# Sums of weight blocks for the MLP's down projection, made by DMAs in device memory

## The chip, the cores and the metric

The kernel runs on one core of one Trainium2 chip. The core has a matrix engine (TensorE, "PE" in the profile; its weight loads are "PEld"), a vector engine (VectorE, DVE), an activation engine (ScalarE, ACT), a general engine (GpSimd, POOL) and a sync engine (SyncE, SP), and 16 DMA engines that all of them share. The metric is the time of one execution on the device, in microseconds (us), lower is better. The change is compared by the median of several runs on the same chip.

## The reference

Two layers, each with attention and an MLP, on 256 tokens of width 1024, in float32. The attention (sparse heads and forgetting heads beside each other) is unchanged here. What the change is about is the MLP:

```
h = _rms_norm(x, g_pre_mlp[l])
y = jnp.square(jax.nn.relu(h @ w_up[l])) @ w_down[l]
x = x + _rms_norm(y, g_post_mlp[l])
```

`w_up` is 1024 x 4096 and `w_down` 4096 x 1024 for each layer.

## The kernel before

**Precision.** Every large product is made of three: a weight is split into a rounded part (`whi`) and the rest (`wlo`), the activations too, and high x high, high x low and low x high are added in PSUM (`mm3`, line 819; each is one matmul of 512 columns in the down projection). The splitting of a weight costs a ScalarE copy (`whi`) and a VectorE subtraction (`wlo`). Some weights, of kind "cast", are split by two DMAs of GpSimd's queue instead, with a ScalarE negation between them (`Weights.cast`, line 589; tile `whic`).

**The units.** All weights stand in one list of units in the order of use (lines 690 to 744): for a layer the six chunks of `w_in` (`("in", c, q)`), eight of `w_out` (`("out", k)`), four of the first up columns, and then, for the MLP, up blocks and rows of `w_down` in turn. Each unit is 512 KB as a rule. SyncE loads them into nine buffers with the tag "raw" (`Weights.load`, line 580), up to 12 units ahead. `Weights.get` (line 604) returns a unit's two parts.

**The MLP.** `up_block` (line 1607) makes 128 hidden columns for all 256 tokens with 8 matmuls of 512 columns and 8 of 256. ScalarE copies half of the PSUM result to `h`, VectorE adds the other half, and `squared` (line 1620) applies a relu and a square on ScalarE. The down projection goes through the hidden columns in pairs of 128-row blocks (loop at line 1735). A pair's four weight blocks and four activation blocks form a 2 x 2 by 2 x 2 block product. The letter N in `PAIRS` (line 100) marks a pair with eight block products, S one with seven, made from sums and differences of the blocks (a Strassen-like scheme). Each layer has 14 such pairs, the first of them N, the others S; the last two pairs of blocks go to `down` directly (line 1776). For an S pair, `operands` (line 1631) makes the activation sums, and `Weights.pair` (line 631) the weight sums: `s` = upper row's two blocks + block b12 of the lower row (one VectorE add of 128 x 1024, line 657), and from it two more (lines 659 and 660). The seven products add up in seven PSUM banks over all pairs; in the last pair `bank_sums` (line 1714) combines the banks as their products end.

**The order.** Nothing is issued in program order. `Recorder` (line 237) records all operations of the program, `schedule` (line 378) simulates the engines with a cost table, and each engine's order is what that simulation gives; an operation's rank is a due time, to which `SHIFTS` (line 38) adds random amounts from listed seeds for listed ranges of operations (`shift`, line 373). On each engine, and on each queue, what is issued later waits behind what is issued earlier. GpSimd's own work is small: its DMAs for cast weights in the MLP and, in attention, the masks of the forget bias (`forget_bias`, line 1203).

Of the kernel before, what the change touches and what calls it, by code (L numbers as in the profile page):

```python
# [17 lines left out]

F32 = mybir.dt.float32
# [17 lines left out]
CAST_HEAD, CAST_TAIL = 1900, 3000.0  # L37
SHIFTS = ((628313922, 3237, 3426, 150),
          (701981142, 3624, 4129, 150),
          (295680985, 724, 994, 400),  # L40
          (1009766576, 3675, 3950, 2500),
          (651636505, 4766, 4926, 1000),
          (434429208, 2775, 3180, 150),
          (330988171, 2766, 2894, 400),
          (958370765, 1025, 1090, 1000),
          (602402177, 3152, 3215, 1000),
          (332536528, 4058, 4926, 400),
          (79554178, 1086, 1213, 2500),
          (824043290, 940, 1079, 1000),
          (929176947, 3864, 4015, 400),  # L50
          (947144828, 4255, 4300, 2500),
          (756884776, 3456, 3727, 2500),
          (352764400, 4430, 4926, 150),
          (731199972, 4142, 4926, 150),
          (788198929, 2312, 2374, 150),
          (633381528, 3971, 4127, 400),
          (189321402, 212, 298, 1000),
          (1057377739, 3585, 3670, 1000),
          (849038195, 2001, 2686, 150),
          (171135740, 3547, 3803, 1000),  # L60
          (797947262, 3731, 4006, 150),
          (383419172, 3908, 4049, 150),
          (230125934, 3754, 4926, 400),
          (705380179, 934, 1003, 1000),
          (185781734, 312, 351, 400),
          (109646568, 3638, 4033, 1000),
          (284246459, 1248, 1293, 2500),
          (664160879, 3832, 3909, 1000),
          (490562272, 1162, 1214, 2500),
          (375550898, 420, 479, 1000),  # L70
          (587899166, 421, 510, 400),
          (501883715, 407, 453, 1000),
          (769019964, 3494, 3544, 2500),
          (369012694, 3554, 3595, 1000),
          (68297707, 3532, 3570, 2500),
          (889231503, 306, 456, 150),
          (1002206527, 1055, 1198, 1000),
          (976623511, 478, 553, 400),
          (608331619, 372, 417, 1000),
          (308090406, 341, 392, 1000))  # L80
LANDING = 2500.0
# [17 lines left out]
            "share", "x0", "x1", "fV", "hs", "cs", "pcT", "vbig", "vS", "vW", "kstk", "kstv", "rT")  # L99
PAIRS = ("NSSSSSSSSSSSSS",) * 2  # L100
DCAST = 1
EPS = 1e-6

CHUNKS = [(512, 1024), (1024, 1312), (0, 512), (1312, 1824), (1824, 2336), (2336, 2848)]
# [132 lines left out]
class Recorder:  # L237
# [135 lines left out]
    def shift(self, seed, a, b, size):  # L373

        for op, x in zip(self.ops[a:b], np.random.default_rng(seed).standard_normal(b - a)):
            op.rank += size * x * (0.01 if op.engine == "tensor" else 1.0)
# [196 lines left out]
class Weights:  # L573


    def __init__(self, nc, tile, units):
        self.nc, self.tile, self.units = nc, tile, units
        self.raw, self.marks, self.ring, self.w1 = {}, [], None, 1

    def load(self, i):  # L580
        kind, shape, src = self.units[i]
        if kind == "raw":
            self.w1 = 1 - self.w1
            self.raw[i] = self.tile([P] + shape, F32, name="w1", tag=f"act{self.w1}", bufs=2)
        else:
            self.raw[i] = self.tile([P] + shape, F32, name="wraw", tag="raw", bufs=RBUFS)
        self.nc.sync.dma_start(self.raw[i], src)

    def cast(self, i):

        nc, marks = self.nc, self.marks
        kind, shape, src = self.units[i]
# [5 lines left out]
        nc.gpsimd.dma_start(hi, src)  # L598
        nc.scalar.activation(lo, hi.bitcast(F32), AF.Copy, scale=-1.0)
        nc.gpsimd.dma_start(lo, src.bitcast(F32R), accum_op=OP.add)  # L600
        nc.key = None
        return hi, lo

    def get(self, i):
# [16 lines left out]
        for j in range(shape[0]) if i < len(FIRSTS) else [slice(None)]:  # L621
            if i > 1:
                nc.scalar.activation(hi[:, j], raw[:, j], AF.Copy)
            else:

                nc.vector.tensor_copy(hi[:, j], raw[:, j])
            nc.vector.tensor_sub(lo[:, j], raw[:, j], hi[:, j].bitcast(F32))
        nc.key = None
        return hi, lo

    def pair(self, i, seven):

        nc, marks = self.nc, self.marks
        for x in (i, i + 1):
            assert len(marks) == x
            marks.append(len(nc.ops))
            if x not in self.raw:
                nc.key = marks[max(x - LOAD_LEAD, 0)]
                self.load(x)
        above, below = (self.raw.pop(x)[:, 0] for x in (i, i + 1))  # L640
        nc.key = marks[max(i - SPLIT_LEAD, 0)]

# [36 lines left out]
def trunk(nc, A, consts_in, out, sbp, pp, dram):  # L679
# [6 lines left out]
    def small(shape, name, bufs=2):  # L686
        return tile(shape, F32, name=name, tag=name, bufs=bufs)
# [17 lines left out]
    for l in range(DEPTH):  # L705
# [22 lines left out]
        def add_up(fc, q):  # L728
            add_unit((l, "up", fc, q), [8, P], A["w_up"][l, 4 * (fc - 1) + q], "cast" if q % 2 else "split")

        def add_down(fc, q, kind):
            add_unit((l, "dn", fc, q), [1, D], wd[:, 4 * fc + q:4 * fc + q + 1, :], kind)

        for u in range(16):
            b, shared = u % 2 * 2, u < len(PAIRS[l])
            if u + 2 < 16 and shared:
                add_up((u + 2) // 2, b)
            if u == len(PAIRS[l]):
                for v in range(4 + 2 * u, 32):
                    add_up(v // 4, v % 4)  # L740
            for i in range(2):
                add_down(u // 2, b + i, "cast" if not shared and (u < 14 or i == DCAST) else "split")
            if u + 2 < 16 and shared:
                add_up((u + 2) // 2, b + 1)

    W = Weights(nc, tile, units)

# [193 lines left out]
    for l in range(DEPTH):  # L941
# [665 lines left out]
        def up_block(fc, b, h):  # L1607
# [106 lines left out]
        def bank_sums(p):  # L1714
# [17 lines left out]
            elif p == 3:  # L1732
                nc.vector.tensor_add(banks[3], banks[3], sums[5])

        for u in range(len(PAIRS[l])):
            fc, b = (u + 2) // 2, u % 2 * 2
            if fc < 8:
                h = tokt("h")
                up_block(fc, b, h)
            if u == 0:  # L1740
                acts.update(enumerate(then()))
            if u == 1:
# [3 lines left out]
            if PAIRS[l][u] == "S":  # L1746
                b11, b22, b21, t1, t2, t3, t4 = w
                work = [(1, 1, b11), (2, 3, b21), (3, 6, b22), (5, 5, t1), (7, 4, t2), (6, 0, t3), (4, 2, t4)]
                if u == len(PAIRS[l]) - 1:
                    work = [work[i] for i in (0, 5, 3, 4, 6, 1, 2)]  # L1750
            else:
                b11, b22, b21, b12 = w
                work = [(2, 1, b11), (4, 0, b11), (5, 0, b12), (3, 4, b12), (2, 3, b21), (4, 2, b21), (5, 2, b22), (3, 5, b22)]
            for n, (p, x, v) in enumerate(work):
                if n == 4 and fc < 8:
                    up_block(fc, b + 1, h)
                    if u + 2 < len(PAIRS[l]):
                        q = blocks(u + 2)
                        squared(q[0][:, 0:4].rearrange("p a n -> p (a n)"), h)
                        acts[u + 2] = operands(u + 2, q)  # L1760
                    else:
                        direct_operands(u + 2, h)
                new = p not in banks
# [5 lines left out]
        ys = {(1, 0): banks[2], (1, 1): banks[3], (0, 0): banks[4], (0, 1): banks[5]}  # L1769
        for v in range(2 + len(PAIRS[l]), 16):  # L1770
            h = tokt("h")
            for i in range(2):
                up_block(v // 2, v % 2 * 2 + i, h)
            direct_operands(v, h)

# [82 lines left out]
```

## Time and profile before

| | |
|---|---|
| median of 3 runs | 598.09 us (598.0 to 598.14) |
| span of the profiled execution | 596.4 us |
| its clock of TensorE, mean | 0.999 |
| device memory read | 132.37 MB |
| device memory written | 1.07 MB |
| mean DMA rate over the span | 225 GB/s |

The profiled execution's own time outside the span isn't listed; the median lies 1.7 us over the span. In rows of the profile, "a<-b" means that the operation writes tile a from tile b; every operation stands at line 498, where the recorded program is emitted, so groups are told apart by their tiles. A row of stretches (such as "579.00:590.00") has the length, the busy time and number of instructions of PE, PEld, DVE, ACT and POOL, the granted clock of TensorE, the DMA engines' mean busy share, and GB/s. The stretches of the layers, by TensorE's products: attention of layer 0 to about 125 us, its MLP to about 297 us, attention of layer 1 to about 420 us, its MLP to 590 us.

### The profile page before, as it was taken

How to read it: one execution, taken by the hardware profiler on the slowest of the kernel's cores; microseconds unless marked ns; L12 is line 12 of the kernel's file. 1: busy time of each engine (PE TensorE's matmuls, PEld its weight loads, DVE VectorE, ACT ScalarE, POOL GpSimd, SP SyncE). 2: the span in 40 equal slices, each digit the busy share in tenths (PEclk: the TensorE clock that was granted, in tenths of full speed). 3: DMA queues.
4: the chain of work that ended last, by engine and by line, in shares of the span. 5: the costliest groups of instructions: out<-in, count | busy, mean ns of one | idle time of the engine just before them, and what ended most of it. 6: DMA issues, size and time to landing. Idle time of an engine off the chain costs nothing.

```text
span 596.4 us, 9853 instructions
## 1 busy us (share of the span) xinstructions
PE 589.1 (99%) x3308; PEld 492.1 (83%) x3308; DVE 542.1 (91%) x1206; ACT 461.4 (77%) x902; POOL 54.0 (9%) x84
## 2 busy tenths in 40 slices
PE   9999999999999999999999999999999999999995
PEld 7978887788888888888888888777888888888884
DVE  6899999879999999998899999986999999999974
ACT  6797878678897787888698658985878878878762
POOL 0001100110011010111000020001100101011110
PEclk9999999999999999999999999999999999999999
DMA  8998128778888989897856481557868899898352
GB/s 315 401 407 290 63 75 293 258 221 222 262 240 270 257 229 281 259 248 211 265 190 234 143 296 59 174 180 248 183 240 240 251 259 232 261 270 220 70 107 70
DMA packets 39858, 134.08 MB, mean 225 GB/s; under 512 B 4704, under 2 KB 5888, under 8 KB 39808
## 3 DMA queue, kind: packets, MB, share of 16 engines
q1 hardware_dynamic: 30592, 99.90, 48.3%
q0 software_dynamic: 9216, 33.56, 25.2%
q8 instruction: 26, 0.43, 0.3%
q14 instruction: 24, 0.20, 0.1%
HBM read 132.37 MB, written 1.07 MB: 224 GB/s over the span
## 4 chain that ended last, share of the span: by engine, by line
PE 98%; DMA 1%; DVE 0%; DVEq 0%; ACT 0%; issue 0%
PE s L498 42%; PE acc L498 26%; PE x L498 20%; PE o L498 10%; DMA first<-in_first_dram 1%; DVE x L498 0%; DVE m L498 0%; DVEq L1854 0%; ACT rl L498 0%; DVE whi L498 0%; DVE rsqrt L498 0%; DVE gcol L498 0%
## 5 line engine op out<-in xcount | busy, mean ns | idle before, releaser
L498 DVE TENSOR_TENSOR wlo<-wraw,whi 128x1024 fp32r<-128x1024 f32 (+2 forms) x156 | 171.1, 1104 | 9.9 <-ACT whi L498 8.4
L498 ACT ACTIVATE whi<-wraw 128x1024 fp32r<-128x1024 f32 (+2 forms) x156 | 149.4, 966 | 29.1 <-PE s L498 13.1
L498 PE MATMUL s<-xT,whic 128*128 128x512 f32 (+1 forms) x448 | 84.0, 336 | 0.0
L498 PEld LDWEIGHTS s<-xT,whic 128*128 128x128 f32 x448 | 72.8, 189 | 10.9
L498 POOL DMA_DIRECT2D whic<-in_w_up_dram x56 | 40.2, 720 | 348.3 <-PE s L498 132.9
L498 DVE TENSOR_TENSOR wlo<-wsum,whi 128x1024 fp32r<-128x1024 f32 x52 | 62.6, 1218 | 1.7 <-ACT whi L498 1.5
L498 ACT ACTIVATE whi<-wsum 128x1024 fp32r<-128x1024 f32 x52 | 53.8, 1054 | 8.2 <-PE acc L498 7.7
L498 PE MATMUL s<-xT,whi 128*128 128x512 f32 x224 | 56.9, 390 | 0.0
L498 PEld LDWEIGHTS s<-xT,whi 128*128 128x128 f32 x224 | 41.8, 188 | 8.5
L498 ACT ACTIVATE attn<-attn,st 128x256 f32<-128x256 f32 (+1 forms) x96 | 42.8, 448 | 5.1 <-DVE st L498 4.7
L498 PE MATMUL x<-whi,aS 128*128 128x512 f32 x120 | 46.4, 390 | 0.0
L498 PE MATMUL acc<-whi,aS 128*128 128x512 f32 x120 | 43.0, 391 | 0.0
L498 ACT ACTIVATE h<-s 128x256 f32<-128x256 f32 x56 | 21.4, 382 | 23.4 <-PE s L498 23.1
L498 PE MATMUL s<-whi,aS 128*128 128x512 f32 x104 | 37.9, 392 | 0.0
L498 PE MATMUL acc<-whi,xT 128*128 128x512 f32 (+1 forms) x128 | 36.2, 349 | 0.0
L498 DVE TENSOR_TENSOR wsum<-wraw,wsum 128x512 f32<-128x512 f32 x52 | 35.5, 683 | 0.1
L498 PE MATMUL x<-whi,xT 128*128 128x512 f32 x112 | 34.7, 391 | 0.3 <-DVE gcol L498 0.3
L498 ACT ACTIVATE whic<-whic 128x1024 fp32r<-128x1024 f32 x32 | 33.5, 1049 | 1.0 <-DMA whic<-in_w_up_dram 1.0
L498 PE MATMUL acc<-xT,whi 128*128 128x512 f32 x128 | 34.1, 398 | 0.0
L498 PEld LDWEIGHTS s<-xT,wlo 128*128 128x128 f32 x224 | 31.2, 190 | 2.5
L498 PE MATMUL s<-xT,wlo 128*128 128x256 f32 x224 | 32.3, 283 | 0.0
L498 DVE TENSOR_TENSOR wsum<-wraw 128x1024 f32<-128x1024 f32 x26 | 31.6, 1216 | 0.0
(236 smaller groups left out, 1321.1 us busy)
## 6 DMA issues: line engine op xcount, KB each, us to landing
wraw<-in_w_down_dram SPq DMA_DIRECT2D x60, 512.0 KB, 5.1
whic<-in_w_up_dram POOLq DMA_DIRECT2D x56, 512.0 KB, 7.1
wraw<-in_w_in_dram SPq DMA_DIRECT2D x36, 512.0 KB, 6.5
wraw<-in_w_up_dram SPq DMA_DIRECT2D x36, 512.0 KB, 4.5
wraw<-in_w_out_dram SPq DMA_DIRECT2D x16, 512.0 KB, 5.2
w<-in_cmp_w_k_dram SPq DMA_DIRECT2D x8, 512.0 KB, 8.2
w<-in_cmp_w_v_dram SPq DMA_DIRECT2D x8, 512.0 KB, 8.9
whic<-in_w_down_dram POOLq DMA_DIRECT2D x8, 512.0 KB, 6.6
```

The lines of the kernel that those rows point to most:

```text
L498: getattr(getattr(self.nc, op.engine), name)(*[real(v) for v in args], **{k: real(v) for k, v in kw.items()})
```

## The change

For some S pairs the sum `s` is made in device memory. `PRE` lists pairs with the weight unit at whose splitting the sum is begun: in layer 0 pairs 0 to 5 from `("in", 5, 1)` to `("out", 2)`, in layer 1 pairs 0 to 11 from `("in", 4, 0)` to `("out", 3)`. Only pairs with the letter S are taken (pair 0 is N), so 5 and 11 sums. At a listed unit GpSimd copies one element of that unit's `wlo` (so its queue waits until the split is done), then issues the accumulation of the sum begun before (b12, read twice, added to both halves), then the copy of this pair's upper row to device memory. In the MLP SyncE loads the sum into a "raw" buffer, and of the lower row only the first half; the VectorE add at line 657 is left out for these pairs. For the other S pairs it stays.

Besides: `up_block`'s add becomes a custom VectorE operation that adds and clamps to the range from 0 to the largest float, so `squared` needs no relu (28 ScalarE operations fewer); the last pair's products come in another order; `SHIFTS` is another list, 11 entries where there were 43. `CASTS`, `HWCAST` and `AHEAD` have values that keep the former behaviour, and the rewritten loops over the up blocks make the same units and products in the same recorded order.

```diff
-SHIFTS = ((628313922, 3237, 3426, 150),
...
+SHIFTS = ((1003350174, 1078, 1222, 2500),
...
+PRE = ([(0, ('in', 5, 1)), (1, ('in', 5, 2)), (2, ('in', 5, 3)), (3, ('out', 0)), (4, ('out', 1)), (5, ('out', 2))], [(0, ('in', 4, 0)), (1, ('in', 4, 1)), (2, ('in', 4, 2)), (3, ('in', 4, 3)), (4, ('in', 5, 0)), (5, ('in', 5, 1)), (6, ('in', 5, 2)), (7, ('in', 5, 3)), (8, ('out', 0)), (9, ('out', 1)), (10, ('out', 2)), (11, ('out', 3))])
...
+    def presum(self, i, seen):
+
+        nc = self.nc
+        nc.gpsimd.tensor_copy(self.tick, seen)
+        nc.after = nc.ops[-1]
+        if self.begun:
+            j, s = self.begun.pop()
+            b12 = self.units[j + 1][2][:, 0, 512:]
+            nc.gpsimd.dma_start(s, bass.AP(b12.tensor, b12.offset, [b12.ap[0], [0, 2], b12.ap[1]]), accum_op=OP.add)
+        if i is not None:
+            s = self.sums[i] = nc.tile(self.dram, [P, 2, 512], F32, name=f"sum{i}")
+            nc.gpsimd.dma_start(s, self.units[i][2][:, 0].rearrange("p (a n) -> p a n", a=2))
+            self.begun.append((i, s))
+        nc.after = None
...
-        self.nc.sync.dma_start(self.raw[i], src)
+        self.nc.sync.dma_start(*[x[:, :, :512] if half else x for x in (self.raw[i], src)])
...
+        if i in self.pre or self.begun:
+            self.presum(self.pre.get(i), lo[0:1, 0, 0:1].bitcast(F32))
...
+        made = seven and i in self.sums
+        if made:
+            nc.key = marks[max(i + 1 - LOAD_LEAD, 0)]
+            s = self.tile([P, 2, 512], F32, name="wsum", tag="raw", bufs=RBUFS)
+            nc.sync.dma_start(s, self.sums.pop(i))
...
-        s, z = (self.tile([P, 2, 512], F32, name="wsum", tag="kx%d" % j) for j in range(2))
-        nc.vector.tensor_add(s, above.rearrange("p (a n) -> p a n", a=2), b12[:, None, :].to_broadcast([P, 2, 512]))
+        z = self.tile([P, 2, 512], F32, name="wsum", tag="kx1")
+        if not made:
+            s = self.tile([P, 2, 512], F32, name="wsum", tag="kx0")
+            nc.vector.tensor_add(s, above.rearrange("p (a n) -> p a n", a=2), b12[:, None, :].to_broadcast([P, 2, 512]))
...
+    pre = {}
+    for l in range(DEPTH):
+        for u, at in PRE[l]:
+            if PAIRS[l][u] == "S":
+                pre[index[(l,) + at]] = index[l, "dn", u // 2, u % 2 * 2]
...
-            nc.vector.tensor_add(d, ps[:, :S], d)
+            nc.vector._custom_dve(op=TENSOR_ADD_SAT, out=d, in0=ps[:, :S], in1=d, s0=FMAX, s1=0.0)
...
-            rl = small([P, 512], "rl")
-            nc.scalar.activation(rl, h, AF.Relu)
-            nc.scalar.activation(d, rl, AF.Square)
+            nc.scalar.activation(d, h, AF.Square)
...
-                    work = [work[i] for i in (0, 5, 3, 4, 6, 1, 2)]
+                    work = [work[i] for i in (0, 5, 1, 3, 4, 6, 2)]
```

More of the change, by code (lines that the diff above doesn't have):

```diff
@@ L17 @@
 from concourse import mybir
+from concourse.dve_ops import TENSOR_ADD_SAT
 F32 = mybir.dt.float32
@@ L37 @@
 CAST_HEAD, CAST_TAIL = 1900, 3000.0
-SHIFTS = ((628313922, 3237, 3426, 150),
[L39 to L80, printed above, removed]
+SHIFTS = ((1003350174, 1078, 1222, 2500),
+          (534435998, 190, 301, 1000),
+          (1036816610, 3033, 3605, 1000),
+          (52205258, 1084, 1186, 1000),
+          (344636226, 190, 635, 400),
+          (407487018, 190, 243, 400),
+          (68684986, 3533, 3578, 2500),
+          (-1, 3555, 3556, -3362),
+          (363124729, 2994, 3063, 400),
+          (811001117, 3517, 3622, 1000),
+          (68206210, 3819, 3828, 2500))
 LANDING = 2500.0
@@ L99 @@
             "share", "x0", "x1", "fV", "hs", "cs", "pcT", "vbig", "vS", "vW", "kstk", "kstv", "rT")
-PAIRS = ("NSSSSSSSSSSSSS",) * 2
+PAIRS = ('NSSSSSSSSSSSSS', 'NSSSSSSSSSSSSS')
+CASTS = ((1, 3), (1, 3))
+HWCAST = 0
+PRE = ([(0, ('in', 5, 1)), (1, ('in', 5, 2)), (2, ('in', 5, 3)), (3, ('out', 0)), (4, ('out', 1)), (5, ('out', 2))], [(0, ('in', 4, 0)), (1, ('in', 4, 1)), (2, ('in', 4, 2)), (3, ('in', 4, 3)), (4, ('in', 5, 0)), (5, ('in', 5, 1)), (6, ('in', 5, 2)), (7, ('in', 5, 3)), (8, ('out', 0)), (9, ('out', 1)), (10, ('out', 2)), (11, ('out', 3))])
 DCAST = 1
 EPS = 1e-6
+AHEAD = 0
+FMAX = 3.4028234663852886e38
 CHUNKS = [(512, 1024), (1024, 1312), (0, 512), (1312, 1824), (1824, 2336), (2336, 2848)]
@@ L373, in shift @@
     def shift(self, seed, a, b, size):
+        if seed < 0:
+            for op in self.ops[a:b]:
+                op.rank += size
+            return
         for op, x in zip(self.ops[a:b], np.random.default_rng(seed).standard_normal(b - a)):
@@ L573, with __init__, load @@
 class Weights:
-    def __init__(self, nc, tile, units):
-        self.nc, self.tile, self.units = nc, tile, units
+    def __init__(self, nc, tile, units, dram, pre):
+        self.nc, self.tile, self.units, self.dram, self.pre, self.sums, self.begun = nc, tile, units, dram, pre, {}, []
+        self.tick = tile([1, 1], F32, name="tick")
         self.raw, self.marks, self.ring, self.w1 = {}, [], None, 1
-    def load(self, i):
+    def presum(self, i, seen):
[11 more added lines that the diff above has]
+        nc.after = None
+    def load(self, i, half=False):
         kind, shape, src = self.units[i]
@@ L597, in cast @@
         nc.key = marks[max(i - CAST_LEAD, 0)]
-        nc.gpsimd.dma_start(hi, src)
-        nc.scalar.activation(lo, hi.bitcast(F32), AF.Copy, scale=-1.0)
+        if HWCAST:
+            self.load(i)
+            raw = self.raw.pop(i)
+            nc.scalar.activation(lo, raw, AF.Copy, scale=-1.0)
+            nc.scalar.activation(hi, raw, AF.Copy)
+        else:
+            nc.gpsimd.dma_start(hi, src)
+            nc.scalar.activation(lo, hi.bitcast(F32), AF.Copy, scale=-1.0)
         nc.gpsimd.dma_start(lo, src.bitcast(F32R), accum_op=OP.add)
@@ L638, in pair @@
                 nc.key = marks[max(x - LOAD_LEAD, 0)]
-                self.load(x)
+                self.load(x, half=seven and i in self.sums and x == i + 1)
         above, below = (self.raw.pop(x)[:, 0] for x in (i, i + 1))
+        made = seven and i in self.sums
[3 more added lines that the diff above has]
+            nc.sync.dma_start(s, self.sums.pop(i))
         nc.key = marks[max(i - SPLIT_LEAD, 0)]
@@ L728, in add_up @@
         def add_up(fc, q):
-            add_unit((l, "up", fc, q), [8, P], A["w_up"][l, 4 * (fc - 1) + q], "cast" if q % 2 else "split")
+            add_unit((l, "up", fc, q), [8, P], A["w_up"][l, 4 * (fc - 1) + q], "cast" if q in CASTS[l] else "split")
         def add_down(fc, q, kind):
             add_unit((l, "dn", fc, q), [1, D], wd[:, 4 * fc + q:4 * fc + q + 1, :], kind)
+        ups = [(1 + j // 4, j % 4) for j in range(28)]
+        for x in ups[:AHEAD]:
+            add_up(*x)
         for u in range(16):
             b, shared = u % 2 * 2, u < len(PAIRS[l])
[L736 to L740, printed above, removed]
+            for x in ups[AHEAD + 2 * u:AHEAD + 2 * u + 1]:
+                add_up(*x)
             for i in range(2):
                 add_down(u // 2, b + i, "cast" if not shared and (u < 14 or i == DCAST) else "split")
-            if u + 2 < 16 and shared:
-                add_up((u + 2) // 2, b + 1)
-    W = Weights(nc, tile, units)
+            for x in ups[AHEAD + 2 * u + 1:AHEAD + 2 * u + 2]:
+                add_up(*x)
+    pre = {}
[3 more added lines that the diff above has]
+                pre[index[(l,) + at]] = index[l, "dn", u // 2, u % 2 * 2]
+    W = Weights(nc, tile, units, dram, pre)
     def weight(*key):
@@ L1733, in bank_sums, with up @@
                 nc.vector.tensor_add(banks[3], banks[3], sums[5])
-        for u in range(len(PAIRS[l])):
[L1736 to L1741, printed above, removed]
+        hs = {}
+        def up(j):
+            if j >= 28:
+                return
+            if j % 2 == 0:
+                hs[j // 2] = tokt("h")
+            up_block(1 + j // 4, j % 4, hs[j // 2])
+            if j == AHEAD:
+                acts.update(enumerate(then()))
+            if j % 2:
+                u = j // 2 + 2
+                if u < len(PAIRS[l]):
+                    q = blocks(u)
+                    squared(q[0][:, 0:4].rearrange("p a n -> p (a n)"), hs[j // 2])
+                    acts[u] = operands(u, q)
+                else:
+                    direct_operands(u, hs[j // 2])
+        for j in range(AHEAD):
+            up(j)
+        for u in range(len(PAIRS[l])):
+            b = u % 2 * 2
+            up(AHEAD + 2 * u)
             if u == 1:
@@ L1754, in trunk @@
             for n, (p, x, v) in enumerate(work):
[L1755 to L1762, printed above, removed]
+                if n == 4:
+                    up(AHEAD + 2 * u + 1)
                 new = p not in banks
@@ L1769, in trunk @@
         ys = {(1, 0): banks[2], (1, 1): banks[3], (0, 0): banks[4], (0, 1): banks[5]}
[L1770 to L1774, printed above, removed]
         def down(t, n, k, w):
```

## The prediction

> **What bounds the kernel now.** I read the page first: the span, the busy times, the chain that ended last.
>
> ```profile
> span 596.4 us, 9853 instructions
> PE 589.1 (99%) x3308; PEld 492.1 (83%) x3308; DVE 542.1 (91%) x1206; ACT 461.4 (77%) x902; POOL 54.0 (9%) x84
> PE 98%; DMA 1%; DVE 0%; DVEq 0%; ACT 0%; issue 0%
> ```
>
> TensorE is busy 99% of the span and the chain is TensorE for 98% of it. But a matmul's end is modelled, so busy does not yet mean that it runs at its rate. The waits of TensorE and the first and last long pieces of the chain come next (start, length, engine and tile, matmuls).
>
> ```profile
> PE o L498 <- PEq L1848: 0.8, 1, 0.8
> PE x L498 <- DVE gcol L498: 0.3, 1, 0.3
> ...
> 4.94 11.56 PE x L498 x48
> ...
> 584.75 5.45 PE acc L498 x24
> ```
>
> It waits 1.1 us in all. The products run from 4.94 us to 590.20 us, 585.3 us; 4.9 us lie ahead (the first load) and 6.2 us behind (norm and store). The change touches neither end. What is left is the rate in between. Here are the same up block in layer 0's MLP, six pairs apart, the product behind it, and the last stretch by engine.
>
> ```profile
> 208.70 2.93 PE L498 MATMUL s<-xT,whic 128*128 128x512 f32 x16
> 211.47 0.40 PE L498 MATMUL s<-whi,aS 128*128 128x512 f32 x1
> ...
> 270.78 2.93 PE L498 MATMUL s<-xT,whic 128*128 128x512 f32 x16
> ...
> 579.00:590.00 11.00, 11.00 (x50) 8.93 (x48) 5.93 (x13) 3.92 (x12) 0.00 (x0) 1.00 0.08 24
> ```
>
> In the last 11 us VectorE works 5.93 us, ScalarE 3.92 us, the DMA engines 8%, and the granted clock is 1.00: nothing there can hold TensorE up. There 24 products of 512 columns take 5.45 us, 227 ns each: I take this as the rate. An up block takes 211.47 - 208.70 = 2.77 us. A pair of seven products with its two up blocks is then 7 x 3 x 0.227 + 2 x 2.77 = 10.31 us. The measured period is (270.78 - 208.70) / 6 = 10.347 us. So **0.04 us per pair, 1 us over the 26 seven-product pairs of both layers, is all that a faster VectorE or ScalarE can give back in the MLP.**
>
> By the Trainium skill (TensorE: Matmul & The Clock Gate, "Wait — 56ns, not 53.3ns?") a warm matmul of 512 columns starts 215.7 ns after the one before. This trace disagrees: 227 ns at full clock, even beside idle engines. Were the 11 ns contention that lighter engines remove in the changed pairs, an estimate by the page would be 16 x 37 x 11 ns = 6.5 us less; by the row, where VectorE and ScalarE do about half of what they do in the MLP and the products stay at 227 ns, it is 0, and I go by the row.
>
> **The change part by part.** The listed pairs are six in layer 0 and twelve in layer 1; each list's first is pair 0, whose letter is N and which the code skips. So 5 + 11 = 16 sums are made, not the 17 of the heading. The products stay seven (eight for pair 0) per pair: TensorE's work is unchanged.
>
> ```profile
> L498 DVE TENSOR_TENSOR wsum<-wraw 128x1024 f32<-128x1024 f32 x26 | 31.6, 1216 | 0.0
> L498 ACT ACTIVATE rl<-h 128x512 f32<-128x512 f32 x28 | 17.3, 617 | 4.0 <-DVE h L498 3.9
> L498 DVE TENSOR_TENSOR h<-s,h 128x256 f32<-128x256 f32 x56 | 23.5, 419 | 3.3 <-ACT h L498 2.7
> L498 DVE CUSTOM_DVE_ANT_0 attn<-x,cst 128x256 f32<-128x256 f32 x32 | 13.3, 417 | 0.4 <-PE s L498 0.4
> ```
>
> Removed: 16 adds of 1216 ns, 19.5 us of VectorE, all in the MLP, and 28 relus of 617 ns, 17.3 us of ScalarE, also there. Both lie beside TensorE, which does not wait for them: at most the 1 us above comes out. I take 0.3 us, a third, since not each lag of a few ns is theirs.
>
> Changed: 56 plain adds become clamping adds, a custom operation that this trace does not have. Another custom operation on the same 128x256 takes 417 ns against 419. Lower end 0; upper end two passes, 56 x 0.42 = 24 us of VectorE. I take 0, by the row of the same size.
>
> Added on the DMA side: per sum a copy of 512 KB from device memory to device memory and an accumulating DMA of 512 KB into it. Later one 512 KB load of the sum, and 256 KB less of the lower row.
>
> ```profile
> q1 hardware_dynamic: 30592, 99.90, 48.3%
> q0 software_dynamic: 9216, 33.56, 25.2%
> ...
> 66.00:100.00 34.00, 34.00 (x215) 27.50 (x216) 32.20 (x119) 28.54 (x87) 0.77 (x2) 1.00 0.41 136
> 100.00:140.00 40.00, 40.00 (x244) 31.68 (x241) 33.68 (x98) 29.50 (x75) 3.55 (x5) 1.00 0.79 234
> ...
> 327.00:376.00 49.00, 49.00 (x359) 40.54 (x357) 47.35 (x155) 34.68 (x89) 3.66 (x8) 1.00 0.48 167
> 376.00:409.00 33.00, 33.00 (x229) 25.11 (x224) 25.82 (x103) 26.88 (x80) 0.26 (x1) 1.00 0.59 191
> 440.00:480.00 40.00, 40.00 (x203) 34.08 (x202) 37.77 (x55) 32.06 (x50) 4.30 (x6) 1.00 0.76 220
> 480.00:520.00 40.00, 40.00 (x207) 34.23 (x206) 39.31 (x58) 32.19 (x43) 5.77 (x8) 1.00 0.90 257
> 520.00:560.00 40.00, 40.00 (x204) 34.16 (x204) 39.17 (x55) 31.62 (x42) 5.74 (x8) 1.00 0.81 208
> ```
>
> GpSimd's queue (q0) moved 64 transfers of 512 KB in 25.2% of 596.4 us: 2.35 us of all 16 engines each. SyncE's (q1) takes 48.3% x 596.4 / 99.90 = 2.88 us per MB, 1.51 us for 512 KB. The trace has no transfer that reads and writes device memory in bulk. Lower end for one: 1.51 us; upper end: 2 x 2.35 us, if both sides count. I take 2.35 us, the queue's own row, so 4.7 us per sum (3.0 to 9.4): 23.5 us in layer 0, **52 us in layer 1** (33 to 103).
>
> Each sum starts when VectorE has split the weight that the list names. Counted back from the first 512-column split (pair 1's, which follows them in the units' order), the first and last of these splits are, for layer 0 and layer 1:
>
> ```profile
> 66.27 1.22 DVE L498 TENSOR_TENSOR wlo<-wraw,whi 128x1024 fp32r<-128x1024 f32 x1
> ...
> 92.72 1.21 DVE L498 TENSOR_TENSOR wlo<-wraw,whi 128x1024 fp32r<-128x1024 f32 x1
> ...
> 327.19 1.23 DVE L498 TENSOR_TENSOR wlo<-wraw,whi 128x1024 fp32r<-128x1024 f32 x1
> ...
> 375.72 1.21 DVE L498 TENSOR_TENSOR wlo<-wraw,whi 128x1024 fp32r<-128x1024 f32 x1
> ```
>
> Free DMA time is one minus the last column but one, times the length. In layer 0 it is 20.1 + 8.4 = 28.5 us from 66 to 140 us: 23.5 us fit. In layer 1 it is 25.5 + 13.5 = **39 us** from 327 to 409, for 52: 13 us of transfers are still to do when the MLP's cast weights begin. The MLP has 9.6 + 4.0 + 7.6 = 21 us free from 440 to 560, of which its larger loads take 11 x 0.75 = 8 us (256 KB each): 13 us are left, so it comes out even at the end. Who waits behind the sums?
>
> ```profile
> 416.85 1.82 POOL L498 DMA_DIRECT2D whic<-in_w_up_dram x2 [6.45 <-ACT whic L498]
> ...
> 436.28 1.77 PE L498 MATMUL s<-xT,whic 128*128 128x512 f32 x7
> ...
> 411.85 0.33 SPq L498 DMA_DIRECT2D wraw<-in_w_down_dram  x1
> 422.16 0.33 SPq L498 DMA_DIRECT2D gains<-in_g_post_mlp_dram  x1
> ...
> whic<-in_w_up_dram POOLq DMA_DIRECT2D x56, 512.0 KB, 7.1
> ...
>   DMA wraw<-in_w_out_dram: 0.6, 1
>   DMA wraw<-in_w_in_dram: 0.5, 2
> ```
>
> On GpSimd's queue it is the first cast weights of layer 1. Their second half is issued at 416.85, lands 7.1 us later by the median, at 424, and is first used at 436.28: 12 us to spare, against 13 us of arrears. On SyncE's queue nothing is issued from 411.85 to 422.16, as no buffer comes free, and in the whole run work on loaded weights waited 1.1 us for a load: these loads are early, by some 10 us, and can give way to the casts. Against the change speaks the Trainium skill (DMA: Bandwidth & Descriptors, "Issuing engines are not separate DMA queues"): transfers of all engines run on the same 16. The shares above agree, near 0.9 in the MLP where both queues work. By that rule the sums take their time from weight loads, and only spare time pays for them.
>
> So the sums cost 0 while 12 + 10 us of cover stand against 13; beyond that, the cost is what is late.
>
> The GpSimd side: each sum adds a one-element copy that waits for VectorE's split of a weight, and behind it stand its two DMAs and, in attention, the 16 masks of the forget bias, which the fox scores need.
>
> ```profile
> POOL bias L498 <- ACT attn L498: 65.9, 1, 65.9
> ...
> 106.56 0.48 PE L498 MATMUL x<-whi,oT 128*128 128x512 f32 x1
> 106.97 0.93 PE L498 MATMUL s<-fkT,fqT 64*128 64x128 f32 x8
> ...
> 576.66 0.70 DVE L498 TENSOR_TENSOR x<-x,s 128x512 f32<-128x512 f32 x1
> ...
> 579.15 0.39 PE L498 MATMUL x<-whi,aT 128*128 128x512 f32 x1
> ```
>
> GpSimd is busy 9% and stands idle 65.9 us before a mask; a copy ahead of it costs nothing unless its weight is later than the mask's turn. Lower end 0, upper end one weight's spacing, 5 us; I take 0.
>
> The sums' load on SyncE waits for the accumulation, and all later loads stand behind it. The planner places the load by when its data is due; I take 0, and if a sum is late, the cost is its lateness.
>
> Last pair: bank 2's products move ahead, so bank 4's sum (0.70 us) ends later before the product that reads it (576.66 + 0.70 against 579.15, 1.8 us spare). Three products, 0.68 us, move away: still covered. 0, at worst 0.7 us twice.
>
> The order: the list of shifts that the planner adds to its ranks is another, so all engines' orders change. The change of tile between products is what an order can save or waste: 106.97 - 106.56 = 0.41 us against 0.227, 0.18 us. About 20 groups of small products enter and leave it, 40 changes, 4 to 7 us in the span. A reorder that merges or parts a fifth moves the time by about 1 us, either way. I take 0.
>
> Sum: 0 - 0.3 + 0 = 0.3 us less: a span of 596.1 us. The median of the runs shown, 598.09, lies 1.7 us over the span; that stays, so **597.8 us**.
>
> **The rivals.**
>
> *The order comes out better.* The 1 us of the MLP and 1 to 2 us of tile changes in attention: 2 us, 596 us. For it: such lags exist. Against: TensorE is at its rate nearly everywhere, so little is left.
>
> *The sums crowd the DMA engines (slower).* Place: layer 1, 409 to 450 us, the cast weights behind eleven sums. It decides from (39 + 22) / 11 = 5.5 us per sum, against my 4.7. At 5.9 us TensorE waits 0.4 x 11, about 4 us: 602 us. For it: most of the way between my bounds lies above. Against: 5.5 us is a sixth over the queue's own row, and a share of 0.5 counts packets that wait.
>
> *The order comes out worse.* More tile changes, a mask behind a waiting copy: 2 us, 600 us.
>
> *The clamping add takes two passes.* Layer 0 has 8 MLP pairs without relief; VectorE, at 39.3 of 40 us in such stretches, gets 0.84 us more per 10.35 and sets the pace: 0.7 us each, near 5 us in all: 603 us.
>
> *The sums are not made as described:* 16, not 17, which is 1.2 us of VectorE off the chain, no time.
>
> **How the numbers follow.** A measurement here tells 0.2%, 1.2 us, from no change: same is 596.9 to 599.3. No change worth telling 0.43; better order 0.30, so faster 0.30; crowded DMAs 0.15, worse order 0.10, slow clamp 0.02, slower 0.27. The range goes from 595.6 (the order's best case and a bit) to 602.5 (crowding as priced): about 0.08 lies below and 0.08 above.
>
> **What would show it.** Right: TensorE's rows at 227 ns and 10.3 us per pair, ten adds of wsum left, no rl beside h, VectorE some 20 us and ScalarE 17 us less busy, the DMA share near 1 from 327 to 440 us, the time unmoved. Wrong: waits of TensorE on cast weights or splits after 410 us; h at 0.8 us; products under 220 ns; an attention that is shorter or longer by over 1.5 us.

## The result: 602.76 us, and where 4.4 us come from

| | before | after |
|---|---|---|
| median of the runs | 598.05 us (598.0 to 598.14, 4 runs) | 602.76 us (601.95 to 602.93, 4 runs) |
| ratio to before | | 1.0073 [1.0061, 1.0085] |
| span of the profiled execution | 596.4 us | 600.8 us |
| its clock of TensorE, mean | 0.999 | 0.994 |

The changed kernel is slower by 0.7%. That is 0.26 us above the upper end of the predicted range and on the side that had a chance of 0.27. The medians differ by 4.7 us, the spans of the two profiled executions by 4.4; the account below is of the spans. All operations of the changed kernel stand at line 476.

The page of the kernel after first: span, busy times, the two DMA queues (packets, MB, share of 16 engines), the chain, and three rows of the DMA issues (KB each, median us to landing).

```profile
span 600.8 us, 9926 instructions
PE 591.2 (98%) x3308; PEld 494.7 (82%) x3308; DVE 526.6 (88%) x1190; ACT 447.2 (74%) x874; POOL 82.9 (14%) x134
...
q1 hardware_dynamic: 32896, 104.09, 48.2%
q0 software_dynamic: 14080, 50.34, 36.0%
...
PE 95%; DMA 4%; ACT 0%; DVE 0%; issue 0%; DVEq 0%
...
sum<-in_w_down_dram POOLq DMA_DIRECT2D x32, 512.0 KB, 12.2
wraw<-in_w_out_dram SPq DMA_DIRECT2D x16, 512.0 KB, 10.0
```

VectorE is 15.5 us less busy and ScalarE 14.2 us less, somewhat under the forecast 20 and 17. But DMA has gone from 1% to 4% of the chain: somewhere a load now sets the end. The 32 `sum` transfers are two for each of 16 sums. The groups of VectorE of the kernel after show the other two edits at the sizes that were expected, 10 adds left of 26 and a clamping add of 420 ns:

```profile
L476 DVE CUSTOM_DVE_ANT_0 h<-s,h 128x256 f32<-128x256 f32 x56 | 23.3, 420 | 4.3 <-ACT h L476 3.7
L476 DVE TENSOR_TENSOR wsum<-wraw 128x1024 f32<-128x1024 f32 x10 | 12.2, 1217 | 0.0
```

Next, in which stage the time is lost. In the chain (start, length, what) the same 16 products stand at the end of layer 0 and at the end of layer 1's attention. Before:

```profile
292.29 3.63 PE acc L498 x16
...
414.31 3.63 PE acc L498 x16
```

After, with the first and the last products:

```profile
5.27 11.75 PE x L476 x48
...
292.69 3.63 PE acc L476 x16
...
419.09 3.64 PE acc L476 x16
...
589.87 4.77 PE acc L476 x21
```

| from, to | before | after | difference |
|---|---|---|---|
| first product | 4.94 | 5.27 | +0.33 |
| layer 0 | 287.35 | 287.42 | +0.07 |
| **layer 1, attention** | 122.02 | 126.40 | **+4.38** |
| layer 1, MLP, to the last product | 175.89 | 175.55 | -0.34 |

The first load, which the change doesn't touch, took 3.93 us instead of 3.60. Layer 0 with its five sums costs nothing, layer 1's MLP has not become longer, and the whole loss is in layer 1's attention. TensorE's waits of the kernel after (us in total, times, longest):

```profile
PE s L476 <- ACT attn L476: 2.3, 1, 2.3
PE o L476 <- PEq L1867: 0.8, 1, 0.8
PE x L476 <- ACT xT L476: 0.3, 1, 0.3
```

One is new, 2.3 us on ScalarE. The chain through it:

```profile
339.24 6.15 PE acc L476 x35
...
345.52 17.26 DMA wraw<-in_w_out_dram
...
362.80 1.06 ACT whi L476
363.86 0.39 ACT attn L476
...
364.29 0.50 PE s L476 x2
```

SyncE issues the load of the second `w_out` weight at 345.52, and it lands 17.26 us later. ScalarE's own timeline of that kernel (start, length, operation; in brackets the idle time before it and its releaser) shows who stands behind it:

```profile
358.62 0.39 ACT L476 ACTIVATE fkT<-acc 128x256 f32<-128x256 f32 x1
362.80 1.06 ACT L476 ACTIVATE whi<-wraw 128x1024 fp32r<-128x1024 f32 x1 [3.80 <-DMA wraw<-in_w_out_dram]
363.76 0.47 ACT L476 ACTIVATE attn<-s 128x384 f32<-128x384 f32 x1
```

The operations of ScalarE run in the order in which they were issued. ScalarE stands for 3.8 us before the split of that weight, and what TensorE waits for is not the weight but the score tile `attn`, which comes next behind the split. Last, the stretches of the kernel after (length, five busy times, granted clock, DMA share, GB/s):

```profile
345.00:350.00 5.00, 5.00 (x57) 3.57 (x55) 4.18 (x15) 2.35 (x8) 2.31 (x5) 1.00 0.81 170
350.00:355.00 5.00, 5.00 (x39) 4.27 (x32) 4.94 (x17) 1.92 (x7) 0.83 (x1) 1.00 1.11 343
362.00:364.00 2.00, 0.02 (x1) 0.00 (x0) 0.67 (x2) 1.20 (x2) 0.07 (x1) 1.00 1.09 299
366.00:367.00 1.00, 1.00 (x7) 1.00 (x6) 0.06 (x2) 0.35 (x1) 1.00 (x4) 0.50 1.08 284
363.00:376.00 13.00, 11.71 (x57) 10.17 (x58) 10.07 (x37) 9.80 (x28) 3.83 (x10) 0.87 1.07 309
```

TensorE does 0.02 us of work from 362 to 364, and soon after it, from 365 us on, the granted clock is 0.50. Over 13 us the mean clock is 0.87, which costs 13 x 0.13 = 1.7 us if all work there goes by the clock. The account of the profiled execution is 2.3 us of wait + 1.7 us of lower clock = 4.0 of the 4.4 us.

Two of these stretches, and the one ahead of them, in the kernel before are rows that the prediction didn't ask for:

```profile
327.00:345.00 18.00, 18.00 (x129) 14.74 (x128) 17.69 (x43) 11.90 (x22) 0.00 (x0) 1.00 0.43 140
345.00:350.00 5.00, 5.00 (x58) 3.54 (x56) 5.00 (x19) 2.43 (x7) 1.35 (x2) 1.00 0.99 312
350.00:355.00 5.00, 5.00 (x36) 4.50 (x33) 4.43 (x13) 2.23 (x5) 1.54 (x4) 1.00 1.03 414
```

For 10 us, while the four bias loads and the first `w_out` weights come in together, the DMA engines had no free time at all before the change (the share adds up the packets' times, so it can come out a little over 1). The mean of 0.48 over 327 to 376 us, from which the prediction took its 25.5 us of free time, hid that.

### The profile page after: what moved, and what is told of

It is laid out like the page before. It is cut to its first block, busy times and chain, and to the rows that moved or that the text cites. A ratio compares the mean times of both kernels' runs of the same rounds, so it can differ in the third digit from the quotient of the medians.

```text
span 600.8 us, 9926 instructions
## 1 busy us (share of the span) xinstructions
PE 591.2 (98%) x3308; PEld 494.7 (82%) x3308; DVE 526.6 (88%) x1190; ACT 447.2 (74%) x874; POOL 82.9 (14%) x134
## 3 DMA queue, kind: packets, MB, share of 16 engines
q0 software_dynamic: 14080, 50.34, 36.0%
## 4 chain that ended last, share of the span: by engine, by line
PE 95%; DMA 4%; ACT 0%; DVE 0%; issue 0%; DVEq 0%
PE s L476 41%; PE acc L476 24%; PE x L476 20%; PE o L476 10%; DMA wraw<-in_w_out_dram 3%; DMA first<-in_first_dram 1%; ACT whi L476 0%; DVE x L476 0%; DVE m L476 0%; DVEq L1873 0%; ACT xT L476 0%; ACT attn L476 0%; DVE rsqrt L476 0%; ACT rl L476 0%; DVE fqT L476 0%
## 5 line engine op out<-in xcount | busy, mean ns | idle before, releaser
L476 DVE TENSOR_TENSOR wlo<-wraw,whi 128x1024 fp32r<-128x1024 f32 (+2 forms) x156 | 171.7, 1106 | 10.1 <-ACT whi L476 7.3
L476 PE MATMUL s<-xT,whic 128*128 128x512 f32 (+1 forms) x448 | 82.4, 336 | 0.0
L476 DVE TENSOR_TENSOR aS<-quads,aS 128x896 fp32r<-128x896 f32 (+3 forms) x30 | 30.5, 1017 | 5.2 <-ACT aS L476 4.9
```

Of the source, the lines that this page charges most:

```text
L476: getattr(getattr(self.nc, op.engine), name)(*[real(v) for v in args], **{k: real(v) for k, v in kw.items()})
```

## The experiments

My theory after the result: the sums in flight at 343 to 363 us meet this burst of loads; one `w_out` weight is late; two engines that take their instructions in order stand behind it; the clock falls. The rivals: the new order of all engines (another `SHIFTS` list) is itself worse; the DMA traffic as a whole, wherever it falls, is too much; the copies block GpSimd's queue.

**1. No sums in layer 1.** Kernel after, its order of instructions kept, at emission:

```diff
+                made = [self.upper[v.buf] for v in op.args if isinstance(v, View) and v.buf in self.upper]
+                if made and made[0][0] >= 5:
+                    if op.engine == "gpsimd":
+                        continue
+                    if op.engine == "sync":
+                        op.args = (op.args[0], made[0][1])
+                        op.bufs = [op.args[0].buf]
```

> The changed kernel in its own order of every engine, but the 22 DMAs of layer 1's eleven sums are not issued; in their place the MLP loads the upper rows alone, at the same size, so the sums lack b12. Theory (crowding): these DMAs make a load of w_out late, ScalarE's queue stands behind its split, TensorE waits 2.3 us and then runs 3.4 us at half clock. Then the wait is gone, w_out lands in 4 to 8 us instead of 17, and the time falls by about 4 us to 598.5 to 599.2. Rival (the new order of the engines is the cost): the wait stays, 602 to 603.

Measured: 597.94 us (597.63 to 598.78) beside 598.38 of before, ratio 0.9995 [0.9986, 1.0005]. The whole loss is gone, and with it the rival of the order: the new order, the clamp and layer 0's five sums together cost nothing. But for the 22 DMAs this kernel has the instructions of the kernel after in the same order, so it also shows how early the late load was. Its timeline (SyncE, then ScalarE) and the DMA line of the view of that load:

```profile
342.87 0.38 SPq L484 DMA_DIRECT2D wraw<-in_w_out_dram  x1
...
358.85 1.05 ACT L484 ACTIVATE whi<-wraw 128x1024 fp32r<-128x1024 f32 x1
...
DMA to landing us min/median/max: 6.6/6.6/6.6
```

Issued at 342.87, landed 6.6 us later at 349.5, split at 358.85: 9.4 us early. In the kernel after the same load is issued at 345.52, 2.65 us later, and takes 17.3 us, 10.7 longer. 2.65 + 10.7 - 9.4 = 3.9 us late, and the split starts 362.80 - 358.85 = 3.95 us later. Why even the issue is later shows in SyncE's timeline of the kernel after:

```profile
339.69 0.63 SPq L476 DMA_DIRECT2D sums<-cs  x2
343.87 0.35 SPq L476 DMA_DIRECT2D bias<-sums  x1
```

The first bias load waits for two transfers of 4 and 8 KB to land, and stands 4.2 us behind them; without the sums it was 1.7 us (339.80 to 341.48). So these two small transfers were delayed as well, and what SyncE issues next stood behind them.

**2. The clamp alone.** Kernel before, with the clamping add and without the relus, no sums. The exchange is made at emission, so the order of before stays:

```diff
+                if op in self.relus:
+                    continue
+                if op in self.squares:
+                    op.args = (op.args[0], self.squares[op]) + tuple(op.args[2:])
+                if op in self.clamp:
+                    d, a, b = map(real, op.args)
+                    self.nc.vector._custom_dve(op=TENSOR_ADD_SAT, out=d, in0=a, in1=b, s0=FMAX, s1=0.0)
+                    continue
```

> The kernel before in its own order, with the clamping add in place of the 56 plain adds and without the 28 relus on ScalarE; no sums in device memory. If TensorE at its rate is the bound: ScalarE 17 us less busy and the time the same, ratio 0.999 to 1.0005. If lighter engines speed it up: ratio below 0.998. If the clamping add takes two passes: its row shows 0.8 us and the ratio is 1.003 or more.

Measured: 598.18 us beside 598.09, ratio 1.0001 [0.9991, 1.001]. ScalarE is 13.5 us less busy (447.9 for 461.4), not quite the 17 of the expectation, and TensorE gains nothing by it. The relief is off the path, as the page of before said.

**3. Four sums less.** As in 1, but only the third to sixth sum of layer 1 are left out, whose eight transfers the kernel after issues from 341.5 to 361.0 us:

```diff
-                if made and made[0][0] >= 5:
+                if made and made[0][0] in (7, 8, 9, 10):
```

> The changed kernel in its own order without the DMAs of four of layer 1's eleven sums, the third to the sixth, whose copies and accumulations lie between 336 and 364 us beside the burst of bias and w_out loads; for these four pairs the MLP loads the upper row alone, so their sums lack b12. Theory (it is the coincidence with that burst): the wait at 362 us is gone, 598 to 599.5. Rival (the total backlog of eleven sums, seven of which remain, delays what comes after): 600 to 603.

Measured: 598.41 us (597.84 to 598.65) beside 598.09, ratio 1.0002 [0.9992, 1.0011]. Seven of eleven sums stay, and the loss is gone. The stretches of this kernel:

```profile
345.00:363.00 18.00, 17.99 (x139) 14.76 (x138) 17.22 (x56) 10.83 (x30) 3.80 (x10) 1.00 0.84 290
363.00:376.00 13.00, 13.00 (x83) 10.87 (x83) 11.46 (x51) 10.01 (x33) 4.66 (x11) 1.00 0.77 278
```

The load is issued at 344.85 and takes 10.1 us instead of 17.3; it lands at 354.95, and its split starts at 358.55: 3.6 us of the cover are left. So the loss hangs on the sums of that time. This run alone doesn't rule out the sum of the traffic over the stage: seven sums of 4.1 us (worked out in the next section) are 29 us and fit in the 39 us that were free from 327 to 409, eleven are 45 and don't. Against it speaks the kernel after itself. The late load landed at 362.78 us, when only 13 of the stage's 22 transfers had been issued, and the other nine can't have held it up.

**4. The traffic in the order of before.** Two kernels: before, with layer 1's copies and accumulations added and their results unused. In the first the accumulation stands directly behind the next weight's tick, in the second four weights behind its copy (the second's lines):

```diff
+        while self.pending and (self.pending[0][2] <= self.turn - 4 or i not in self.pre):
+            b12, s, _ = self.pending.pop(0)
+            g.dma_start(s, bass.AP(b12.tensor, b12.offset, [b12.ap[0], [0, 2], b12.ap[1]]), accum_op=OP.add)
+        if i in self.pre:
...
+            g.dma_start(s, up[:, 0].rearrange("p (a n) -> p a n", a=2))
+            self.pending.append((low[:, 0, 512:], s, self.turn))
```

> The kernel before in its own order, to which only the DMAs of layer 1's eleven sums are added, each behind the split of the listed weight; nothing uses them. If the traffic is the cost in any order: a load of w_out lands 8 to 12 us later, its split, which the kernel before makes at 357 to 361 us, is late, and the time rises by 2 to 5 us to 600 to 603. If it needs the new order: 598 to 598.7.

Measured: 622.16 us beside 598.38, ratio 1.04 [1.0384, 1.0416]; far from what either theory expected, for a reason that neither had. The waits of GpSimd and of TensorE in this kernel:

```profile
POOL sum L512 <- DMA sum<-in_w_down_dram: 79.7, 11, 11.8
...
PE s L500 <- ACT xT L500: 14.6, 1, 14.6
```

An accumulation must wait until its copy has landed. GpSimd's queue stood 79.7 us before its eleven, and everything else of that queue with it: the first cast weight came late, and TensorE waited 14.6 us. That is the price of a place on an in-order queue, not of bandwidth, so this run doesn't decide the question. The second comes closer.

> The kernel before in its own order plus the DMAs of layer 1's eleven sums, as in e4, but each accumulation is issued four weights after its copy, so that GpSimd's queue doesn't wait for copies to land and the masks and cast weights behind them aren't held up. If e4's 24 us were GpSimd's queue: the wait of 14.6 us goes. If the traffic itself costs in this order too: 599.5 to 603, with a late w_out load; if the kernel before's order leaves its loads time enough: 598.2 to 599.

Measured: 602.53 us beside 598.09, ratio 1.0076 [1.0061, 1.0091], the same as the change itself (1.0073). The chain of this kernel and its largest wait of TensorE:

```profile
346.27 16.62 DMA wraw<-in_w_out_dram
...
362.98 1.06 ACT whi L500
```

```profile
PE s L500 <- ACT pcT L500: 1.9, 1, 1.9
```

Another order, no sum used by anybody, and again a load of `w_out` lands 16.6 us after its issue and holds up ScalarE's split at 363 us. It is the third weight here, not the second, and the tile that TensorE lacks is `pcT`, not `attn`. So layer 1's traffic alone is enough for a loss of this size in the old order too; that the sizes agree so closely is partly chance, since three more waits of 0.5 to 0.6 us stand beside this one. The chains of this kernel and of the kernel after hold no operation of GpSimd, so its queue isn't the cause there.

**5. The link between load and TensorE.** If ScalarE's place in line is the link, the late split must cost less when it stands further back. Kernel after, in the finished order, the split of the second `w_out` weight behind n further ScalarE operations, with the subtraction that needs it as far back as that asks, and in the second kernel the subtraction also behind r further VectorE operations (the second's lines):

```diff
+            for i in self.late:
+                for a, e, n in zip(self.splits[i], ("scalar", "vector"), (5, 4)):
+                    p = out.index(a)
+                    q = [j for j in range(p + 1, len(out)) if out[j].engine == e][n - 1]
+                    moved, kept = [a], []
+                    for op in out[p + 1:q + 1]:
+                        (moved if any(d in moved for d in op.deps) else kept).append(op)
+                    out[p:q + 1] = kept + moved
```

> The changed kernel with all its DMAs; in layer 1 the split of the second weight of w_out is moved behind eight operations on ScalarE (and its subtraction behind the operations of VectorE issued until then). Theory (the wait is ScalarE's queue standing behind a split whose weight is late, not a product that needs the weight): TensorE's wait at 362 us goes or falls under 1 us, the clock stays up, 598.8 to 600.5. Rival (products need the late weight, or the next load is as late and stops the queue as long): 602 to 603.

Measured, with n = 8: 603.39 us (600.58 to 604.94) beside 598.38, ratio 1.0077 [1.0052, 1.0102]; no gain. TensorE's wait on ScalarE at 362 us is gone, but another has come four us later:

```profile
PE x L486 <- DVE st L486: 2.1, 1, 2.1
```

The edit moved the split past the point at which VectorE's queue reaches the subtraction that needs it, so VectorE stood instead, with `st` behind it. The expectation had looked at one queue only.

> The changed kernel with all its DMAs; in layer 1 the split of w_out's second weight is moved behind five operations of ScalarE, and its subtraction behind four further operations of VectorE, so that neither queue stands before a late load. Theory (the cost is two queues standing in order behind one late weight): no wait of TensorE over 1 us between 355 and 372 us, the clock stays up, 598.5 to 600.5. Rival (the wait only moves to the next late load): 602 to 604.

Measured, with n = 5 and r = 4: 600.12 us (598.99 to 602.55) beside 598.09, ratio 1.0038 [1.0025, 1.0052]. All DMAs are as in the kernel after, the `w_out` loads land after 18.1 us by the median (18.4 in the kernel after, both from 327 to 409 us), and the DMA share from 345 to 363 is 0.98. Yet of the wait this is left:

```profile
PE x L486 <- DVE st L486: 0.3, 1, 0.3
```

The loads are as late as in the kernel after, and more than half of the loss is gone by the medians: the link is the two in-order queues, and the weight was needed less urgently than its place in line said. The profiled execution was the fastest of the seven (598.99 us); what the slower ones, up to 602.55 us, still lose isn't known.

**6. Shorter packets.** Kernel after, with the sums' rows 4224 bytes apart in device memory, so that a copy can't be made as one contiguous block:

```diff
-            s = self.sums[i] = nc.tile(self.dram, [P, 2, 512], F32, name=f"sum{i}")
+            s = nc.tile(self.dram, [P, 1056], F32, name=f"sum{i}")
+            s = self.sums[i] = s[:, :1024].rearrange("p (a n) -> p a n", a=2)
```

> The changed kernel with each sum's rows 4224 bytes apart in device memory instead of 4096, so that the copy can't be cut into 16 pieces of 32 KB and goes in 128 of 4 KB; same bytes, same order. Theory A (the long packets, 1.2 to 2.1 us each, hold up SyncE's 4 KB packets in each DMA engine): w_out lands earlier, the wait of TensorE shrinks or goes, 598.5 to 601. Theory B (it is the bytes): the load stays at 15 to 18 us, 602 to 603.

Measured: 599.72 us (598.46 to 600.52) beside 598.38, ratio 1.0023 [1.0013, 1.0033]. GpSimd's queue on the page of this kernel (packets, MB, share):

```profile
q0 software_dynamic: 15872, 50.34, 36.5%
```

The same megabytes as in the kernel after, in 15872 - 14080 = 1792 packets more, 112 for each of 16 copies. If a copy now goes in 128 rows of 4 KB, it went in 16 packets of 512 / 16 = 32 KB in the kernel after. The pages agree: of 8 KB and more there are 307 packets in the kernel after, 51 here, and 307 - 51 = 256 is 16 for each of 16 sums. One of these takes 1.2 us in the trace by the median, a 4 KB packet of SyncE's loads 0.16. The chain shows what this does to the load:

```profile
346.78 13.48 DMA wraw<-in_w_out_dram
```

13.5 us instead of 17.3, at the same share (1.03 from 345 to 363 us). TensorE's wait shrinks from 2.3 to 0.2 us in the profiled execution (598.97 us, faster than the median), and by the medians two thirds of the loss are gone. So the layout that gave long packets was a good part of how the sums held up the loads. How it did so is open: from 343 to 363 us both queues moved more than in the kernel after, SyncE's 2.61 MB for 2.35 and GpSimd's 3.28 for 3.07, so the loads didn't just win what the sums lost. The edit also moves the rows in memory, and no run sets the two apart.

**7. Both remedies, and another place.** The first kernel joins 5 (n = 5, r = 4) and 6. The second is the kernel after with another list for layer 1, the planner's order made anew:

```diff
-[(0, ('in', 4, 0)), (1, ('in', 4, 1)), (2, ('in', 4, 2)), (3, ('in', 4, 3)), (4, ('in', 5, 0)), (5, ('in', 5, 1)), (6, ('in', 5, 2)), (7, ('in', 5, 3)), (8, ('out', 0)), (9, ('out', 1)), (10, ('out', 2)), (11, ('out', 3))]
+[(0, ('in', 4, 0)), (1, ('in', 4, 1)), (2, ('in', 4, 2)), (3, ('out', 1)), (4, ('out', 2)), (5, ('out', 3)), (6, ('out', 4)), (7, ('out', 5)), (8, ('out', 6)), (9, ('out', 7))]
```

> The kernel after with both partial remedies: the sums' rows stand 4224 bytes apart in device memory, so that the copies go in 4 KB pieces, and the split of the second w_out weight of layer 1 stands behind five ScalarE operations and its subtraction behind four VectorE operations. All 16 sums are made. Theory (one late weight that two in-order queues stand behind is the whole cost): no wait of TensorE over 0.5 us in layer 1's attention, clock 0.998 or more, 597.9 to 599.0 us. Rival (a part of the cost is the DMA engines' load itself and stays whatever stands behind the weight): 599.5 to 600.5 us, as with either remedy alone (599.72 and 600.12).

Measured: 599.42 us (598.55 to 600.36) beside 598.18, ratio 1.0018 [1.0009, 1.0028]: between the two expectations and hardly better than either remedy alone. In layer 1's attention two small waits of TensorE are left:

```profile
PE x L486 <- DVE st L486: 0.5, 1, 0.5
PE s L486 <- DVE pcs L486: 0.4, 1, 0.4
```

The profiled execution was the slowest of the eleven (600.36 us). Its attention in layer 1 is 1.9 us longer than before the change (its 16 products start at 292.75 and 416.63 us), and these waits are 0.9 us of that; where the rest lies isn't known. Whether the waits would go with a third move, or are a cost of the DMA engines' load as such, this run doesn't tell.

> The kernel after with another list for layer 1: pairs 1 and 2 as before, then nothing until the second w_out weight is split, and pairs 3 to 9 at the w_out units 1 to 7; 9 sums in layer 1 instead of 11, pairs 10 and 11 add on VectorE. The planner makes the order anew. Theory (what costs is that sums in flight meet the burst of bias and w_out loads): the w_out loads land in under 10 us by the median, no wait of TensorE over 1 us before 400 us, 597.9 to 599.2 us, the order's own scatter in it. Rival (the sums need their DMA time somewhere, and later they crowd the MLP's weights, as the prediction had it): a wait on cast weights or masks after 400 us, 600 us or more.

Measured: 601.43 us (600.75 to 602.72) beside 598.18, ratio 1.0057 [1.0045, 1.007]; the first half of the expectation held and the second didn't. The attention is cured: its end, the 16 products, starts at 414.74 (414.31 before the change), and the DMA engines' load is light where the burst lies, with `w_out` loads that land after 6.7 us by the median (327 to 409 us); the sums' time comes behind it, with a share of 1.04 from 376 to 409:

```profile
345.00:363.00 18.00, 18.00 (x142) 15.05 (x141) 16.67 (x64) 11.84 (x34) 3.48 (x8) 1.00 0.71 252
363.00:376.00 13.00, 13.00 (x88) 10.62 (x88) 12.45 (x51) 10.84 (x35) 1.45 (x4) 1.00 0.39 124
```

```profile
wraw<-in_w_out_dram SPq DMA_DIRECT2D x8, 512.0 KB, 6.7
```

But the last product ends at 593.35 us (590.20 before), 2.7 us of it lost in the MLP. TensorE's waits there, and the chain into the second of them:

```profile
PE s L476 <- DVE h L476: 1.7, 2, 1.1
```

```profile
465.03 7.89 DMA whic<-in_w_up_dram
```

The 0.6 us at 478 us lies behind a cast weight that landed 7.9 us after its issue. Cast weights are somewhat late here (8.2 us by the median from 409 to 480, 6.3 before the change), but the last transfer of a sum was issued at 413.09 and landed 14.0 us later, so no sum was in flight then. The 1.1 us at 433.8 stands behind VectorE's splits in the new order, and no wait on a DMA shows next to it. Whether the sums or the planner's other order make these two waits is open. No complete version of the change is faster than before, and with TensorE busy in 99% of the span none could be by much.

## Why the prediction was wrong, step by step

- **TensorE at its rate, relief worth 0.3 us.** Right. Layer 1's MLP is 0.34 us shorter, layer 0 0.07 longer, and the clamp alone brings nothing (2). Differences this small can't be told from scatter: the first load alone moved by 0.33.
- **16 sums, not 17; the clamping add at the price of the plain one; the order, the last pair and the ticks at 0.** Right: 10 adds left of 26, 420 ns, 597.94 us with layer 1's sums taken out (1). The bounds for these steps were far wider than what came.
- **Layer 0's sums fit.** Right, by 1 and by layer 0's length.
- **4.7 us of DMA time for a sum.** About right. GpSimd's queue took 36.0% x 600.8 = 216 us; less the 64 old transfers at 2.35 us, 66 us are left for 32 new ones, 2.06 us each, 4.1 us a sum. That is 45 us for eleven. The 13 us still to do at 409 didn't come: the share from 409 to 440 us is 0.64, less than the 0.85 before.
- **"39 us from 327 to 409, for 52".** The step that failed. Free time was added up over 82 us, as if a sum could use it wherever it lay. But at 345 to 355 us the share was 0.99 and 1.03 before the change. Cut there, the row shows it: up to 355 us 18 x 0.57 = 10.3 us were free, and by 350 us the kernel after has issued ten transfers for sums, the first at 330.24 and the tenth at 349.79, which take 10 x 2.06 = 20.6 us. By this estimate 10 us were missing, and the load issued in between took 10.7 us longer.
- **"These loads are early, by some 10 us, and can give way".** The size was right: 9.4 us for the load in question (1). But the step set this cover, together with the casts' 12 us, against the arrears of the whole stage. One load must be covered by its own 9.4 us, and it was held up by 13.3.
- **The rival of crowded DMA engines.** Direction and cause (loads late through the sums' traffic) were right, with a chance of 0.15. That its price came so near (602 us forecast, 602.76 measured) is luck, since it was worked out for 5.9 us a sum and for another wait. Its place was wrong: not the cast weights behind eleven sums at 409 to 450, where no wait arises, but a `w_out` weight at 362. Its point of decision, 5.5 us a sum over the stage, was wrong with it: at 4.1 us a sum the kernel already loses.
- **What stands behind a late load.** The prediction named it for GpSimd's queue and for SyncE's, not for ScalarE's. There it decides: the score tile behind the split, not the weight, stopped TensorE.
- **The clock.** Not foreseen; 1.7 of the 4.4 us in the profiled execution, by the account above.

## What to carry to other kernels

Before you add transfers, cut the DMA share at the bursts of the loads that are there, not at the stages: where it is already 1, as for 10 us here, new transfers make loads late (10.7 us here), however much is free in the mean. For each load in such a burst find its slack (issue, landing, first use) and what stands in line behind its first use on an in-order engine, since that, not the load's own user, may stop the engine that matters. Off-path engine time that is saved by traffic is a bad exchange where the engine that bounds the kernel gets nothing from it.

## What the runs showed of the hardware that was not expected

- A contiguous copy of 512 KB within device memory went in 16 packets of 32 KB, and a load that ran beside such copies took 17.3 us, beside packets of 4 KB 13.5 us (6). The Trainium skill (DMA: Bandwidth & Descriptors, "Queues, rings and completion order") says that a DMA engine turns between its queues after whole packets; the load's time in this pair of runs agrees in direction. That both queues moved more with the short packets doesn't follow from it.
- An idle time of 2.3 us of TensorE was followed by some 3 us at a granted clock of 0.50. Waits of 2.1 us (the first kernel of 5), 1.9 us (the second of 4) and 1.7 us (the first of 4) were followed by 0.50 as well; waits of 0.2 to 1.1 us were not. The Trainium skill (TensorE: Matmul & The Clock Gate, "Why this matters for your kernels") puts the limit at gaps of more than about 3 us; here shorter ones were enough, and the measurement decides. It doesn't come each time: in one of the four runs of the kernel after the mean clock stayed at 0.999, and its span was 600.0 instead of 600.8 us, which is less of a gain than 1.7. What that run lost instead isn't known, as it wasn't profiled.
- GpSimd's queue stood 79.7 us for eleven accumulations, each waiting for its own copy to land (4). With each accumulation four weights behind its copy the same queue stood 9.0 us for them.
